# Three edits in the embedding stages of an eight-core decoder trunk: FFN tiles interleaved, norm sums on 32-column tiles, last norm shared with GpSimd

## The chip, the cores and the metric

The kernel is one launch on all eight cores of one Trainium2 chip. The metric is device time in microseconds (us) of the slowest core. TensorE does the matmuls, VectorE and GpSimd do elementwise work, ScalarE does activations and squares, and SyncE issues the output DMAs.

The chip lowers the TensorE clock of some cores in some executions. The runs list the mean granted clock of every core. A run is called slow when one die is clearly longer at a lower clock, and slow runs are left out. Even among fast runs some cores lose 0.5 to 1% of their clock. Most of this document compares *stages of one core at full clock*, that is, without such a lowering. Their times agree between cores within about 0.1 us, except in the sample block of stage two and the tail (up to 0.6 and 0.3 us).

## The reference

One inference step of a two-layer trunk with `D_MODEL` 1024 and `D_FF` 2816. Each core has one prompt of 2048 tokens and one eighth of the 1024 sample tokens. Cut to what matters:

```python
for i in range(2):
    x = x + 0.5 * swiglu(rmsnorm(x, norm_ffn[i, 0]), w_ffn_gate_up[i, 0], w_ffn_down[i, 0])
    x = x + mixer(rmsnorm(x, norm_mix[i]))
    x = x + 0.5 * swiglu(rmsnorm(x, norm_ffn[i, 1]), ...)
    # the embedding stage
    gate = sigmoid(rmsnorm(x, norm_ple[i]) @ w_ple_gate[i])
    emb  = rmsnorm(p[i] @ w_ple_proj[i], norm_ple_proj[i])
    x = x + gate * emb
y = rmsnorm(x, norm_final)
```

Every embedding stage is followed by a norm: the first by that of layer 1's FFN, the second by `norm_final`, which is the output.

## The kernel before

A core holds `x` in five blocks: `b` 0 to 3 are 512 prompt tokens each, `b` 4 (`SB`) is 128 sample tokens. Channels lie on the 128 partitions, in eight chunks (`c`, `mo`). So a norm's sum over channels is a sum over partitions: ScalarE squares a chunk, and TensorE multiplies the squares by a 128x128 matrix of ones (`ONES`, holding 1/1024), which leaves the mean in every partition of a PSUM bank.

```python
class Norm:                                    # mode "pe" alone shown
    def square():
        sq = SQ.get()
        act(sq[:, 0:n], xs, AF.Square)                         # ScalarE
        defer(self.wait * k, lambda: add(sq), self.tag)        # placed later
    def add(sq):
        if i == 0: self.pb = bank()
        mm(self.pb[:, 0:n], [(ONES[:, :], sq[:, 0:n])], start=i == 0, stop=i == 7)
        if i == 7: self.rsqrt()
    def rsqrt(self):
        rs = scr()                                             # in SBUF
        act(rs[:, 0:n], self.pb[:, 0:n], AF.Abs_reciprocal_sqrt, bias=NORM_EPS)
        def f():                                               # for c = 0..7, deferred
            out = X if self.final else H
            dve_stt(out[b][:, c, :], X[b][:, c, :], pcol(self.gname, c), rs[:, 0:n], ALU.mult, ALU.mult)
            if self.final:
                dma("sp", d_yT[:, o_:o_ + n], X[b][:, c, :], "osem")

def ple(l, gnext, ahead):                      # the embedding stage of layer l
    for mo, b in order:                        # blocks 0 and 1 mixed, then 2, 3, SB
        if mo == 0:
            if b == SB: advance(ahead, 3)      # three tiles of the next FFN
            ...
            nm[b] = Norm(b, gnext, "pe")
        mm(pz[:, 0:n], [... 8 gate matmuls ...])
        mm(pe_[:, 0:n], [... 2 embedding matmuls ...])
        act(th[:, 0:n], pz[:, 0:n], AF.Tanh, scale=0.5)
        dve_stt(th, th, 1.0, pe_, ALU.add, ALU.mult)
        dve_stt(X[b][:, mo, :], th, GPPH[...], X[b][:, mo, :], ALU.mult, ALU.add)
        nm[b].chunk(mo, 2.8)
```

The square root is in another activation table than the tanh, so each norm costs ScalarE two table loads of 1.28 us. And each of the eight norm multiplies reads two operands in SBUF, `X` and `rs`.

Of the kernel before, what the change touches and what calls it, by code (L numbers as in the profile page):

```python
# [9 lines left out]
AF = mybir.ActivationFunctionType  # L10
ALU = mybir.AluOpType
# [7 lines left out]
NSAMP = NS * TS  # L19
# [5 lines left out]
SB = NB - 1  # L25
NORM_EPS = 1e-6
# [329 lines left out]
def build_program():  # L356
# [37 lines left out]
    X = [alloc(f"x{b}", [128, 8, BLK[b]], F32, f"x{b}") for b in range(NB)]  # L394
# [4 lines left out]
    HID = [at(f"hid{b}", [128, NHP, BLK[b]], BF16, "hid", hid0 + NHP * 2 * BOFF[b], True) for b in range(NB)]  # L399
# [28 lines left out]
    ONES = alloc("ones", [128, 128], BF16)  # L428
# [19 lines left out]
    def pcol(name, c=0, n=1):  # L448
        return PAR[:, PCOL[name] + c:PCOL[name] + c + n]
# [6 lines left out]
    def defer(delay, fn, tag=None):  # L456
        seq[0] += 1
        heapq.heappush(pend, (pe_t[0] + delay, seq[0], tag, fn))
# [33 lines left out]
    def act(out, in_, func, bias=None, scale=None):  # L492
        kw = {}
        rd = [in_]
        if bias is not None:
            kw["bias"] = bias
            if not isinstance(bias, float):
                rd.append(bias)
        if scale is not None:
            kw["scale"] = scale  # L500
            if not isinstance(scale, float):
                rd.append(scale)
        tset = "abs_reciprocal_sqrt_and_small" if func == AF.Abs_reciprocal_sqrt else "silu_and_others"
        keep = func in (AF.Square, AF.Copy, AF.Identity)

        def fn(e):
            if not keep and tset != act_set[0]:
                e.preload_act_table_set(tset)  # L508
                act_set[0] = tset
            return e.activation(out=out, in_=in_, func=func, **kw)  # L510
        S.op("act", fn, reads=rd, writes=[out])
# [3 lines left out]
    def dve_tt(out, in0, in1, op):  # L515
        S.op("dve", lambda e: e.tensor_tensor(out=out, in0=in0, in1=in1, op=op), reads=[in0, in1], writes=[out])

    def pool_tt(out, in0, in1, op):
        S.op("pool", lambda e: e.tensor_tensor(out=out, in0=in0, in1=in1, op=op), reads=[in0, in1], writes=[out])  # L519

    def dve_stt(out, in0, scalar, in1, op0, op1):
        rd = [in0, in1] + ([] if isinstance(scalar, float) else [scalar])
        S.op("dve", lambda e: e.scalar_tensor_tensor(out=out, in0=in0, scalar=scalar, in1=in1, op0=op0, op1=op1),  # L523
             reads=rd, writes=[out])
# [22 lines left out]
    def mm_ops(ops):  # L547
        run_due()

        def fn(e):  # L550
            ins = None
            for i, (o_, l, r, st, sp) in enumerate(ops):
                ins = e.matmul(o_, l, r, start=st, stop=sp)  # L553
                if i == 0 and PE_FW[0] is not None:
                    ins._wait_ge(*PE_FW[0])
                    PE_FW[0] = None
            return ins
        rd = [a for op in ops for a in op[1:3]]
        wr = []
        for op in ops:  # L560
            if not any(op[0] is w for w in wr):
                wr.append(op[0])
        S.op("pe", fn, reads=rd, writes=wr)
# [7 lines left out]
    def mm(out, pairs, start=True, stop=True):  # L571
        n = len(pairs)
        mm_ops([(out, l, r, start and i == 0, stop and i == n - 1) for i, (l, r) in enumerate(pairs)])
        pe_t[0] += sum(max(width(r), 64) + 6.5 for _, r in pairs) / 2400.0
# [87 lines left out]
    class Norm:  # L662
        def __init__(self, b, gname, mode="dve"):
            self.b, self.gname, self.mode = b, gname, mode
            self.final = gname == "norm_final"
            self.n = BLK[b]
            self.tag = ("n", b)
            self.nsq = self.nadd = 0
            self.wait = {"pe": 4.0, "dve": 1.2, "pool": 1.0}[mode]

        def chunk(self, mo, lag=0.8):
            n, xs = self.n, X[self.b][:, mo, :]
            k = 1.0 if n == 512 else 0.4
            add_tt = pool_tt if self.mode == "pool" else dve_tt

            def square():
                self.nsq += 1
                if self.mode != "pe" and self.nsq == 1:
                    self.acc = scr()
                    act(self.acc[:, 0:n], xs, AF.Square)  # L680
                    return
                sq = SQ.get()
                act(sq[:, 0:n], xs, AF.Square)
                defer(self.wait * k, lambda: add(sq), self.tag)

            def add(sq):
                i = self.nadd
                self.nadd += 1
                if self.mode == "pe":
                    if i == 0:  # L690
                        self.pb = bank()
                    mm(self.pb[:, 0:n], [(ONES[:, :], sq[:, 0:n])], start=i == 0, stop=i == 7)
                    SQ.put(sq)
                    if i == 7:
                        self.rsqrt()
                elif i < 6:
                    add_tt(self.acc[:, 0:n], self.acc[:, 0:n], sq[:, 0:n], ALU.add)
                    SQ.put(sq)
                else:
                    add_tt(sq[:, 0:n], self.acc[:, 0:n], sq[:, 0:n], ALU.add)  # L700
                    sfree(self.acc)
                    defer({512: 2.5, NSAMP: 9.0}[n] + (1.5 if self.mode == "pool" else 0.0), lambda: stats(sq), self.tag)

            def stats(sq):
                self.pb = bank()
                mm(self.pb[:, 0:n], [(ONES[:, :], sq[:, 0:n])])
                SQ.put(sq)
                self.rsqrt()

            defer(lag * k, square, self.tag)  # L710

        def rsqrt(self):
            n, b = self.n, self.b
            rs = scr()
            act(rs[:, 0:n], self.pb[:, 0:n], AF.Abs_reciprocal_sqrt, bias=NORM_EPS)
            bfree(self.pb)
            st = 0.7 if n == 512 else 0.3

            def mk(c):
                def f():  # L720
                    out = X if self.final else H
                    dve_stt(out[b][:, c, :], X[b][:, c, :], pcol(self.gname, c), rs[:, 0:n], ALU.mult, ALU.mult)
                    if c == 7:
                        sfree(rs)
                    if self.final:
                        o_ = 8 * BOFF[b] + c * n
                        dma("sp", d_yT[:, o_:o_ + n], X[b][:, c, :], "osem")
                return f
            for c in range(8):
                defer(2.0 + st * c, mk(c), self.tag)  # L730
# [161 lines left out]
    def advance(gen, n=None):  # L892
        while gen is not None and n != 0:
            try:
                next(gen)
            except StopIteration:
                return
            n = None if n is None else n - 1
# [286 lines left out]
    def ple(l, gnext, ahead):  # L1185
        wp = kview(W.get(("plep", l)), 2)
        order = [(mo, b) for b in range(2) for mo in range(3)] + [(mo, b) for b in range(2) for mo in range(3, 8)]
        order += [(mo, b) for b in range(2, NB) for mo in range(8)]
        nm = {}
        for mo, b in order:  # L1190
            n = BLK[b]
            if mo == 0:
                if b == SB:
                    advance(ahead, 3)
                ensure(("n", b))
                ensure(("pt", b))
                nm[b] = Norm(b, gnext, "pe")
            ch = [c for c in TRI if mo in c][0]
            wt = kview(W.get(("pleg", l, ch)), 8)
            ii = ch.index(mo)  # L1200
            pz, pe_ = bank(), bank()
            mm(pz[:, 0:n], [(wt[:, k, ii * 128:(ii + 1) * 128], H[b][:, k, :]) for k in range(8)])
            mm(pe_[:, 0:n], [(wp[:, k, mo * 128:(mo + 1) * 128], HID[b][:, k, :]) for k in range(2)])
            th = scr()
            act(th[:, 0:n], pz[:, 0:n], AF.Tanh, scale=0.5)
            bfree(pz)
            dve_stt(th[:, 0:n], th[:, 0:n], 1.0, pe_[:, 0:n], ALU.add, ALU.mult)
            bfree(pe_)
            dve_stt(X[b][:, mo, :], th[:, 0:n], GPPH[:, l * 8 + mo:l * 8 + mo + 1], X[b][:, mo, :],
                    ALU.mult, ALU.add)  # L1210
            sfree(th)
            nm[b].chunk(mo, 2.8)
        W.done(("plep", l))
        for ch in TRI:
            W.done(("pleg", l, ch))
# [133 lines left out]
```

## Time and profile before

The median was 2630.95 us (2630.5 to 2632.32, three runs). The profiled execution was shorter, 2625.39 us; its slowest core's span is 2623.8 us.

| | us |
|---|---|
| TensorE busy | 2569.3 of 2623.8 |
| first embedding stage, with the FFN tiles run ahead in it | 128.33 |
| second embedding stage, first to last matmul | 91.16 |
| of it blocks 0 to 2, block 3, sample block | 56.77, 20.88, 13.52 |
| tail, last matmul to the end | 13.67 |

The stages are measured in each core's trace between named matmuls, as the median of the cores. These are the head, part 1 and the first line of part 4 (the chain of work that ended last) of the page of the kernel before.

```profile
span 2623.8 us, 34956 instructions; the slowest of 8 cores (2617.4 to 2623.8 us)
PE 2569.3 (98%) x14375; PEld 1245.7 (47%) x14375; DVE 1154.5 (44%) x2039; ACT 708.4 (27%) x1257; POOL 168.0 (6%) x254
...
PE 88%; DVE 5%; ACT 2%; DMA 2%; issue 1%; SPq 1%; POOL 0%; ACTq 0%; DVEq 0%; POOLq 0%
```

TensorE is the limit over the whole kernel. These are the largest waits of TensorE in the second stage, on core 0 of the kernel before (engine, line, what it waited for; us in total, times, longest us).

```profile
PE ps L553 <- DVE scr_95 L523: 3.1, 1, 3.1
PE ps L553 <- DVE scr_96 L523: 1.5, 1, 1.5
```

The TensorE timeline of the same core (start, duration, engine, line, operation, count; in brackets the idle time before it and what ended that) shows where two of such waits lie: the first three lines are block 3 of the first stage, the last the sample block of the second.

```profile
1274.58 1.90 PE L553 MATMUL ps<-h_51,ring 128*128 128x512 bf16 x8
1276.53 0.59 PE L553 MATMUL ps<-hid_56,ring 128*128 128x512 bf16 x2
1278.61 1.90 PE L553 MATMUL ps<-h_51,ring 128*128 128x512 bf16 x8 [1.49 <-DVE scr_96 L523]
...
2601.54 1.04 PE L553 MATMUL ps<-h_52,ring 128*128 128x128 bf16 x8 [3.09 <-DVE scr_95 L523]
```

In the tail, VectorE multiplies the last chunks of block 3 (128x512) and of the sample block (128x128), and SyncE issues one DMA for each. The VectorE and SyncE timelines of core 0, before:

```profile
2612.13 0.61 DVE L523 SCALAR_TENSOR_TENSOR x_47<-x_47,par,scr_93 128x128 f32<-128x128 f32 x2
2612.65 0.75 DVE L523 SCALAR_TENSOR_TENSOR x_46<-x_46,par,scr_95 128x512 f32<-128x512 f32 x1
...
2618.03 1.87 SPq L577 DMA_DIRECT2D yT<-x_46  x4
```

A 128x512 multiply takes 0.75 us, a 128x128 one 0.35, and an issue about 0.48 from start to start.

### The profile page before, as it was taken

To read this page: it belongs to the slowest core of one execution; us is meant where nothing else is said; L and a number is where in the kernel's file an instruction comes from. 1 tells how busy PE (TensorE), PEld (TensorE's weight loads), DVE (VectorE), ACT (ScalarE), POOL (GpSimd) and SP (SyncE) were. 2 spreads that over 40 slices of the span, in tenths; PEclk is the share of its full clock that TensorE was granted. 3 is DMA by queue.
4 is the path that set the end of the run, shared out by engine and by line. 5 is a ranking of instruction groups with operands and counts; after the bars stand their busy time and mean duration, and the time that the engine had idled before them with its cause. 6 is when DMAs were issued, how large, how long until landed. Compare 5 with 4: busy or idle time off the path is not lost.

```text
span 2623.8 us, 34956 instructions; the slowest of 8 cores (2617.4 to 2623.8 us)
## 1 busy us (share of the span) xinstructions
PE 2569.3 (98%) x14375; PEld 1245.7 (47%) x14375; DVE 1154.5 (44%) x2039; ACT 708.4 (27%) x1257; POOL 168.0 (6%) x254
## 2 busy tenths in 40 slices
PE   7999999999899999999999999999999999999997
PEld 3544544444454454444444454445444544544443
DVE  5432344755632222258732222267667322222687
ACT  5210112336621001124521001123334210011254
POOL 0000000012300000000000000000005000000000
PEclk9999999999999999999999999999999999999998
DMA  8220321146341123112042031102310320322113
GB/s 199 51 45 1 65 45 25 24 100 120 78 74 33 25 39 54 29 29 50 1 77 41 17 57 33 33 13 42 61 33 8 57 53 17 57 37 41 21 22 137
DMA packets 53311, 127.18 MB, mean 48 GB/s; under 512 B 9504, under 2 KB 24608, under 8 KB 53024
## 3 DMA queue, kind: packets, MB, share of 16 engines
q0 software_dynamic: 23584, 92.55, 20.4%
q1 hardware_dynamic: 28848, 31.29, 4.4%
q8 instruction: 113, 1.85, 0.3%
q10 hardware_dynamic: 720, 1.11, 0.1%
q14 instruction: 46, 0.38, 0.0%
HBM read 196.61 MB, written 10.62 MB: 79 GB/s over the span
## 4 chain that ended last, share of the span: by engine, by line
PE 88%; DVE 5%; ACT 2%; DMA 2%; issue 1%; SPq 1%; POOL 0%; ACTq 0%; DVEq 0%; POOLq 0%
PE ps L553 88%; SPq L577 1%; DMA ring<-wts 1%; ACT L508 1%; DVE h_50 L523 1%; DVE x_46 L523 0%; DVE h_51 L523 0%; DMA x_43<-xT 0%; DMA rr<-u 0%; DVE h_48 L523 0%; DVE h_49 L523 0%; POOL scr_96 L519 0%; DVE x_45 L523 0%; DVE x_43 L523 0%; DVE scr_93 L523 0%
## 5 line engine op out<-in xcount | busy, mean ns | idle before, releaser
L553 PE MATMUL ps<-h_48,ring 128*128 128x512 bf16 x1892 | 429.6, 380 | 14.4 <-DMA ring<-wts 14.4
L553 PE MATMUL ps<-h_51,ring 128*128 128x512 bf16 x1892 | 427.8, 380 | 3.2 <-DVE scr_96 L523 3.0
L553 PE MATMUL ps<-h_49,ring 128*128 128x512 bf16 x1892 | 427.7, 379 | 1.9 <-DVE h_49 L528 1.4
L553 PE MATMUL ps<-h_50,ring 128*128 128x512 bf16 x1892 | 426.2, 379 | 1.5 <-DVE h_50 L523 1.5
L553 PEld LDWEIGHTS ps<-h_51,ring 128*128 128x128 bf16 x1892 | 185.0, 98 | 228.0 <-DVE scr_96 L523 4.0
L553 PEld LDWEIGHTS ps<-h_50,ring 128*128 128x128 bf16 x1892 | 184.7, 98 | 225.3 <-DVE h_50 L523 2.0
L553 PEld LDWEIGHTS ps<-h_49,ring 128*128 128x128 bf16 x1892 | 184.4, 98 | 225.0 <-DVE h_49 L528 3.8
L553 PEld LDWEIGHTS ps<-h_48,ring 128*128 128x128 bf16 x1892 | 181.4, 98 | 220.1 <-issue 14.6
L577 POOL DMA_DIRECT2D ring<-wts x152 | 80.8, 538 | 2048.6 <-PE ps L553 1960.7
L553 PE MATMUL ps<-hid_56,ring 128*128 128x512 bf16 x736 | 163.8, 379 | 0.0
L553 PE MATMUL ps<-hid_54,ring 128*128 128x512 bf16 x736 | 163.7, 379 | 0.0
L553 PE MATMUL ps<-hid_55,ring 128*128 128x512 bf16 x736 | 163.7, 379 | 0.0
L553 PE MATMUL ps<-hid_53,ring 128*128 128x512 bf16 x736 | 162.8, 379 | 0.0
L510 ACT ACTIVATE scr_94<-ps 128x512 f32<-128x512 f32 (+1 forms) x109 | 61.6, 565 | 323.2 <-PE ps L553 322.9
L510 ACT ACTIVATE scr_97<-ps 128x512 f32<-128x512 f32 (+1 forms) x134 | 69.8, 521 | 282.4 <-PE ps L553 274.8
L510 ACT ACTIVATE scr_96<-ps 128x512 f32<-128x512 f32 (+1 forms) x120 | 68.5, 571 | 237.4 <-PE ps L553 235.2
L510 ACT ACTIVATE scr_95<-ps 128x512 f32<-128x512 f32 (+1 forms) x131 | 68.6, 524 | 234.8 <-PE ps L553 234.5
L553 PE MATMUL ps<-h_52,ring 128*128 128x128 bf16 x1892 | 124.5, 221 | 4.6 <-DVE scr_95 L523 3.1
L553 PEld LDWEIGHTS ps<-h_52,ring 128*128 128x128 bf16 x1892 | 115.3, 99 | 27.5 <-DVE scr_95 L523 3.3
L553 PEld LDWEIGHTS ps<-hid_56,ring 128*128 128x128 bf16 x736 | 72.0, 98 | 86.8
L553 PEld LDWEIGHTS ps<-hid_54,ring 128*128 128x128 bf16 x736 | 72.0, 98 | 86.6
L553 PEld LDWEIGHTS ps<-hid_55,ring 128*128 128x128 bf16 x736 | 72.0, 98 | 86.6
(490 smaller groups left out, 2171.8 us busy)
## 6 DMA issues: line engine op xcount, KB each, us to landing
ring<-wts POOLq DMA_DIRECT2D x110, 512.0 KB, 8.4
ring<-wts POOLq DMA_DIRECT2D x40, 768.0 KB, 6.4
rr<-u SPq DMA_DIRECT2D x48, 135.0 KB, 5.3
rr<-u SPq DMA_DIRECT2D x16, 134.8 KB, 3.5
x_44<-xT SPq DMA_DIRECT2D x8, 256.0 KB, 6.2
x_45<-xT SPq DMA_DIRECT2D x8, 256.0 KB, 11.2
x_46<-xT SPq DMA_DIRECT2D x8, 256.0 KB, 11.6
yT<-x_43 SPq DMA_DIRECT2D x8, 256.0 KB, 2.1
```

Source lines behind the costliest of these rows:

```text
L508: e.preload_act_table_set(tset)
L510: return e.activation(out=out, in_=in_, func=func, **kw)
L523: S.op("dve", lambda e: e.scalar_tensor_tensor(out=out, in0=in0, scalar=scalar, in1=in1, op0=op0, op1=op1), reads=rd, writes=[out])
L553: ins = e.matmul(o_, l, r, start=st, stop=sp)
L577: S.op(eng, lambda e: e.dma_start(out=out, in_=in_), reads=[in_], writes=[out], dma_sem=sem, dma_total=total, extra_deps=extra)
```

## The change

Three things, with three intents. **Tiling:** an accumulation over eight chunks makes TensorE read 8x512 columns for one row of sums. A 32-column tile of the array can sum a chunk on its own, and four such tiles hold four chunks side by side; so blocks 0 to 2 use two groups of four, and then combine the four partial sums. **Interleaving:** three more tiles of the next FFN run inside block 3 of the first stage, to give TensorE work while VectorE catches up. **Sharing:** for the last norm of prompt blocks, GpSimd does three of the eight multiplies; as the instruction used there multiplies two tensors and leaves no place for the gain, ScalarE multiplies the gain in beforehand.

```diff
+            self.shared = (2, 4, 6) if self.final and b < SB else ()
...
+            def tiled():                       # after every four squares
+                mm_ops([(self.pb[32 * q:32 * q + 32, 0:n], ONES[:, 0:32], HID[self.b][:, 3 + 4 * g + q, :], g == 0,
+                         g == 1) for q in range(4)])
+                if g == 1:
+                    hi, lo = self.hl
+                    act(hi[:, 0:n], self.pb[:, 0:n], AF.Copy)
+                    dve_tt(lo[:, 0:n], self.pb[:, 0:n], hi[:, 0:n], ALU.subtract)
+                    defer({512: 5.0, NSAMP: 2.5}[n], combine, self.tag)
+            def combine():
+                mm(self.pb[:, 0:n], [(ONES[:, :], t[:, 0:n]) for t in self.hl])
+                self.rsqrt()
...
+                if mo in self.shared:
+                    act(xs, xs, AF.Copy, scale=pcol(self.gname, mo))
...
-                    dve_stt(out[b][:, c, :], X[b][:, c, :], pcol(self.gname, c), rs[:, 0:n], ALU.mult, ALU.mult)
+                    if c in self.shared:
+                        pool_tt(X[b][:, c, :], X[b][:, c, :], rs[:, 0:n], ALU.mult)
+                    else:
+                        dve_stt(out[b][:, c, :], X[b][:, c, :], pcol(self.gname, c), rs[:, 0:n], ALU.mult, ALU.mult)
...
-                nm[b] = Norm(b, gnext, "pe")
+                nm[b] = Norm(b, gnext, "tile" if b < 3 else "pe")
+            if b == 3 and mo in (3, 5, 7):
+                advance(ahead, 1)
```

Cut: the housekeeping of buffers (tiled blocks keep their squares in free rows of `HID`), and the square root's `scale=32.0` (each partial sum stands in 32 partitions and is divided by 1024 a second time). `hi` and `lo` split the partial sums into two bfloat16 values, so that combining loses little precision.

More of the change, by code (lines that the diff above doesn't have):

```diff
@@ L667, in __init__ @@
             self.tag = ("n", b)
+            self.shared = (2, 4, 6) if self.final and b < SB else ()
             self.nsq = self.nadd = 0
-            self.wait = {"pe": 4.0, "dve": 1.2, "pool": 1.0}[mode]
+            self.wait = {"pe": 4.0, "tile": 5.0, "dve": 1.2, "pool": 1.0}[mode]
         def chunk(self, mo, lag=0.8):
@@ L674, in chunk, with square_ @@
             add_tt = pool_tt if self.mode == "pool" else dve_tt
+            def tiled():
+                g = self.nadd
+                self.nadd += 1
+                if g == 0:
+                    self.pb = bank()
+                mm_ops([(self.pb[32 * q:32 * q + 32, 0:n], ONES[:, 0:32], HID[self.b][:, 3 + 4 * g + q, :], g == 0,
+                         g == 1) for q in range(4)])
+                pe_t[0] += (n + 26) / 2400.0
+                if g == 1:
+                    self.hl = [SQ.get(), SQ.get()]
+                    hi, lo = self.hl
+                    act(hi[:, 0:n], self.pb[:, 0:n], AF.Copy)
+                    dve_tt(lo[:, 0:n], self.pb[:, 0:n], hi[:, 0:n], ALU.subtract)
+                    bfree(self.pb)
+                    defer({512: 5.0, NSAMP: 2.5}[n], combine, self.tag)
+            def combine():
+                self.pb = bank()
+                mm(self.pb[:, 0:n], [(ONES[:, :], t[:, 0:n]) for t in self.hl])
+                for t in self.hl:
+                    SQ.put(t)
+                self.rsqrt()
             def square():
+                square_()
+                if mo in self.shared:
+                    act(xs, xs, AF.Copy, scale=pcol(self.gname, mo))
+            def square_():
                 self.nsq += 1
+                if self.mode == "tile":
+                    act(HID[self.b][:, 2 + self.nsq, :], xs, AF.Square)
+                    if self.nsq % 4 == 0:
+                        defer(self.wait * k, tiled, self.tag)
+                    return
                 if self.mode != "pe" and self.nsq == 1:
@@ L714, in rsqrt @@
             rs = scr()
-            act(rs[:, 0:n], self.pb[:, 0:n], AF.Abs_reciprocal_sqrt, bias=NORM_EPS)
+            act(rs[:, 0:n], self.pb[:, 0:n], AF.Abs_reciprocal_sqrt, bias=NORM_EPS,
+                scale=32.0 if self.mode == "tile" else 1.0)
             bfree(self.pb)
```

## The prediction

> **What bounds the kernel.** TensorE. The page gives PE 98% busy of a 2623.8 us span, and 88% of the chain of work that ended last; the granted clock is 0.994. The change touches only the two embedding stages (about 1216-1316 us and 2519-2610 us in the PE timeline) and the tail after them. There the PE timeline has 512-column matmuls every 0.216 us without gaps, except these stalls, all behind VectorE. Stage one: 1.49 us in block 3, then 0.51, 0.76, 0.46 and 0.48 in the sample block (3.7 us). Stage two: 1.49 us in block 3, 0.64 and 3.09 us in the sample block, and behind the 3.09 a half-clock stretch (8 sample matmuls every 0.83 us instead of 0.45) that costs about 2 us. The 3.09 and 1.49 stalls come from VectorE: in its timeline it waits 3.2 us for ScalarE (two 1.28 us table loads around each norm's square root) and then works off a backlog with eight 0.67 us norm multiplies mixed in. The tail, from the last matmul to the end, is 13.5 us; its 16 output DMA issues stand one behind the other every 0.48 us.
>
> **What the change does to TensorE.** Per block of 0 to 2, eight ones-matmuls (8 x 0.216 = 1.73 us) become two groups of four 32-column matmuls plus two combining ones. The Trainium skill, page "TensorEngine Tiling (Array Packing)", section "Key Properties", says that changing the tiling mode drains TensorE, and that column tiles run in parallel. The trace agrees: the convolution's 32-column groups of four cost 0.22 us each, with about 0.1 us more on entering and on leaving. So 2 x 0.42 + 0.43 = 1.26 us, a gain of 0.47 us per block, 2.8 us over six. It lies on the path, since TensorE has no gaps there. The norms end some 6 us later, which nobody waits for, except that block 2's last norm moves into the sample block.
>
> **Interleaving.** Six FFN tiles run before the sample block instead of three; nothing is added. Each is 3.45 us of TensorE for one 0.7 us VectorE operation, so block 3's 1.49 us stall goes. The sample block's 2.2 us stay mostly: block 3's norm still falls there. Gain 1.5 to 2.
>
> **Last norm shared.** Three of eight multiplies per prompt block leave VectorE (2 us per block); ScalarE pays three copies of about 0.6 us and GpSimd three multiplies of 1.15 us or more. The Trainium skill, page "GPSIMD Engine Reference", table in section 1, says that SBUF interfaces are shared with VectorE and contended with two SBUF inputs; the trace agrees: five norm multiplies took 0.92 us each beside GpSimd work, which then took 1.7. So about half of the relief remains. It removes the 1.49 us stall of block 3 and part of the 3.09 and of the half clock: 3 us (1 to 6), the later norm of block 2 working against it. The tail stays bound by the DMA issues: 0.6 us.
>
> **Sum.** 2.8 + 1.7 + 3 + 0.6, about 8 us: 2623 us, range 2617.5 to 2629. Faster by over 2%: 0.005; within 2%: 0.99; slower: 0.005.
>
> **Right or wrong in the profile.** 32-column groups of 0.3 to 0.45 us start to start; no stall over 1 us in either block 3; the sample block of stage two shorter by 1 to 4 us at full clock; still about 13 us after the last matmul, with issues every 0.48 us.
>
> **What would make it wrong.** Column groups that don't overlap (0.8 us each) would turn the gain into a loss. Table loads of block 2's later norm just before the sample block could starve TensorE there again. GpSimd contention could slow VectorE by as much as it relieves.

## The result, and the profile after

The changed kernel took 2631.93 us (median of four runs, 2630.63 to 2633.4), the kernel before 2631.64 us (2630.5 to 2632.41) beside it. The ratio of the fast runs is 1.0002, with a 95% interval of 0.9984 to 1.0019: the same. Ratios here are the mean time of one kernel's fast runs over that of the other's in the same rounds, so they are not quite the ratio of the quoted medians. The predicted 2623.0 us, and its range of 2617.5 to 2629, were missed.

The first suspicion must be the clock. The views of all cores (median of each die) are, before and then after:

```profile
die 0 (median of its cores): 2621.4 us, clock 0.994
die 1 (median of its cores): 2621.8 us, clock 0.995
```

```profile
die 0 (median of its cores): 2621.7 us, clock 0.994
die 1 (median of its cores): 2628.1 us, clock 0.990
```

Die 1 did lose clock in the changed kernel's four runs. But die 0, at the same clock in both, shows no gain either: 2621.7 against 2621.4 us. So the missing 8 us are not hidden by the clock. They are missing in the stages:

| core at full clock, us | stage 1 | stage 2 (blocks 0-2 / block 3 / sample) | tail | sum |
|---|---|---|---|---|
| before | 128.33 | 91.16 (56.77 / 20.88 / 13.52) | 13.67 | 233.16 |
| after (die 0) | 126.62 | 90.15 (55.22 / 20.21 / 14.72) | 15.99 | 232.76 |
| difference | -1.71 | -1.01 | +2.32 | -0.40 |

The long stretch between the stages is the same in every kernel, 1174.90 us. From the page after:

```profile
PE 2563.0 (97%) x14133; PEld 1245.7 (47%) x14387; DVE 1155.2 (44%) x2033; ACT 719.4 (27%) x1275; POOL 182.8 (7%) x266
```

The weight loads rose by 12, as the change adds two matmuls to each of six norms; that the matmuls seem to have fallen by 242 means that records are missing from this trace. VectorE's busy time did not fall, although 12 multiplies were taken from it and only 6 small subtractions added; GpSimd's rose by 14.8 us for 12 instructions. The waits of TensorE in stage two, core 0 after:

```profile
PE ps L553 <- DVE scr_94 L523: 1.9, 2, 1.5
PE ps L553 <- ACT scr_95 L510: 1.5, 1, 1.5
PE ps L553 <- ACT sq_91 L510: 1.1, 1, 1.1
```

The one wait of 3.1 us has become several smaller ones, some of them for ScalarE. TensorE's timeline after shows the column groups (`ones 128*32`), first one within a stretch without a wait, then one in the first stage that waits for VectorE:

```profile
1239.66 1.89 PE L553 MATMUL ps<-h_49,ring 128*128 128x512 bf16 x8
1241.48 0.40 PE L553 MATMUL ps<-hid_53,ones 128*32 128x512 bf16 x4
1241.81 0.61 PE L553 MATMUL ps<-hid_54,ring 128*128 128x512 bf16 x2
...
1271.70 0.40 PE L553 MATMUL ps<-hid_55,ones 128*32 128x512 bf16 x4 [1.22 <-DVE scr_93 L523]
```

The group takes 0.33 us from start to start, with 0.09 us more ahead of it: 1239.66 plus eight times 0.216 is 1241.39, not 1241.48. That is 0.42 us, as predicted. And this is the tail after, from the VectorE, GpSimd and SyncE timelines of core 0:

```profile
2609.12 0.75 DVE L523 SCALAR_TENSOR_TENSOR x_46<-x_46,par,scr_97 128x512 f32<-128x512 f32 x1
2609.79 3.89 DVE L523 SCALAR_TENSOR_TENSOR x_47<-x_47,par,scr_94 128x128 f32<-128x128 f32 x3
...
2609.23 4.30 POOL L519 TENSOR_TENSOR x_46<-x_46,scr_97 128x512 f32<-128x512 f32 x3 [11.16 <-ACT scr_97 L510]
...
2611.21 2.87 SPq L577 DMA_DIRECT2D yT<-x_47  x3
...
2617.25 2.46 SPq L577 DMA_DIRECT2D yT<-x_46  x5
```

Three VectorE multiplies of 128x128, which took 0.61 us for two before, take 3.89 us here, while GpSimd works through its three. SyncE, which follows VectorE in order, issues three DMAs in 2.87 us.

The sizes behind those sums are in the view of one source line (count, then nanoseconds least, median, most). Before and after, the same multiply:

```profile
L523 DVE SCALAR_TENSOR_TENSOR x_47<-x_47,par,scr_93 x8: 347/347/348, 2612.1 to 2616.0; 128x128 f32<-128x128 f32 x8
```

```profile
L523 DVE SCALAR_TENSOR_TENSOR x_47<-x_47,par,scr_94 x3: 1344/1345/1351, 2609.8 to 2612.3; 128x128 f32<-128x128 f32 x3
```

**Theory.** Tiling pays on TensorE where TensorE is the limit. Sharing gives that back in the tail, because an instruction of VectorE with two SBUF operands cannot run beside GpSimd's: it waits for GpSimd's whole instruction. Interleaving does nothing for the stall it aimed at. **Rivals.** In the tail: GpSimd's multiply is slow in itself and its result arrives late (dependence), or the output queue is the limit. In the sample block of stage two: the later norm of block 2, with its table loads, against TensorE merely arriving earlier at work that VectorE and ScalarE set the pace of.

### The profile page after: what moved, and what is told of

Read it like the earlier page. It is cut to its first block, busy times and chain, and to the rows that moved or that the text cites. A ratio compares the mean times of both kernels' runs of the same rounds, so it can differ in the third digit from the quotient of the medians.

```text
span 2631.9 us, 34689 instructions; the slowest of 8 cores (2617.2 to 2631.9 us)
## 1 busy us (share of the span) xinstructions
PE 2563.0 (97%) x14133; PEld 1245.7 (47%) x14387; DVE 1155.2 (44%) x2033; ACT 719.4 (27%) x1275; POOL 182.8 (7%) x266
## 4 chain that ended last, share of the span: by engine, by line
PE 89%; DVE 4%; ACT 2%; DMA 2%; issue 1%; SPq 1%; POOL 0%; DVEq 0%; ACTq 0%; POOLq 0%
PE ps L553 89%; SPq L577 1%; ACT L508 1%; DVE h_50 L523 1%; DMA x_43<-xT 0%; DVE x_46 L523 0%; DMA xscr_69<-st_sc 0%; DMA rr<-u 0%; DVE h_48 L523 0%; POOL scr_96 L519 0%; DVE h_49 L523 0%; DMA x_44<-xT 0%; DMA ring<-wts 0%; DVE x_45 L523 0%; DVE x_47 L523 0%
## 5 line engine op out<-in xcount | busy, mean ns | idle before, releaser
L553 PEld LDWEIGHTS ps<-h_49,ring 128*128 128x128 bf16 x1892 | 185.7, 98 | 229.2 <-issue 16.4
L553 PEld LDWEIGHTS ps<-h_50,ring 128*128 128x128 bf16 x1892 | 185.1, 98 | 227.0 <-issue 9.4
L553 PEld LDWEIGHTS ps<-h_51,ring 128*128 128x128 bf16 x1892 | 185.2, 98 | 225.8 <-issue 6.9
L553 PEld LDWEIGHTS ps<-h_48,ring 128*128 128x128 bf16 x1892 | 182.1, 98 | 222.0 <-issue 24.4
L510 ACT ACTIVATE scr_96<-ps 128x512 f32<-128x512 f32 (+1 forms) x124 | 70.5, 569 | 370.2 <-PE ps L553 366.5
L510 ACT ACTIVATE scr_97<-ps 128x512 f32<-128x512 f32 (+1 forms) x131 | 69.1, 527 | 284.9 <-PE ps L553 277.4
L510 ACT ACTIVATE scr_95<-ps 128x512 f32<-128x512 f32 (+1 forms) x131 | 68.3, 521 | 234.8 <-PE ps L553 234.8
L553 PEld LDWEIGHTS ps<-h_52,ring 128*128 128x128 bf16 x1892 | 115.4, 99 | 25.8 <-DVE scr_94 L523 1.9
L553 PEld LDWEIGHTS ps<-hid_56,ring 128*128 128x128 bf16 x736 | 72.0, 98 | 86.7
L553 PEld LDWEIGHTS ps<-hid_55,ring 128*128 128x128 bf16 x736 | 71.9, 98 | 86.8 <-issue 0.5
L553 PEld LDWEIGHTS ps<-hid_54,ring 128*128 128x128 bf16 x736 | 71.7, 98 | 86.9 <-issue 1.8
L553 PEld LDWEIGHTS ps<-hid_53,ring 128*128 128x128 bf16 x736 | 71.6, 98 | 84.1 <-issue 0.2
```

Source lines behind the costliest of these rows:

```text
L510: return e.activation(out=out, in_=in_, func=func, **kw)
L553: ins = e.matmul(o_, l, r, start=st, stop=sp)
```

## The experiments

All kernels gave correct results. Stages are given as in the table above; the edits are against the changed kernel unless said otherwise. Where one look is quoted as a time, its profile fell in the fast state; where the kernel before beside it was slow (2938 us in the first group), only stages are compared.

### Tiling alone

```diff
-            self.shared = (2, 4, 6) if self.final and b < SB else ()
+            self.shared = ()
-            if b == 3 and mo in (3, 5, 7):
-                advance(ahead, 1)
```

> Only the column tiling of the square sums is kept; no interleaving, no sharing. Measured on the four cores of the die at full clock, before and after are: first embedding stage (with the twelve or nine lead FFN tiles after it) 128.3 and 126.6 us; second stage 91.2 and 90.15 us, of it blocks 0 to 2 56.8 and 55.2, block 3 20.9 and 20.2, sample block 13.5 and 14.7; tail after the last matmul 13.7 and 16.0. My theory: the tail's loss of 2.3 us comes from the sharing alone (GpSimd and VectorE shut each other out of SBUF), so the tail is 13.7 (13.2 to 14.2) here. Rival: the tail's loss comes from the later end of the tiled norms, which pushes block 2's output writes into the tail; then it stays near 16. First stage: tiling saves 12 matmuls of 0.216 less 12 mode changes of 0.1, 1.4 us, so 126.9 (126.4 to 127.4) if no new stall comes with it.

Measured (one look, 2624.5 us): stage 1 126.19, stage 2 91.48 (56.51 / 19.31 / 15.67), tail 13.48, sum 231.15: 2.0 us less than before. The tail is back, so the tail's loss is not the tiling's. Stage 1 gained 2.14 us. Stage 2 gained nothing: blocks 0 to 2 are only 0.26 us shorter, block 3 is 1.57 us shorter, and the sample block 2.15 us longer. At the end of blocks 0 to 2 a column group now waits for VectorE, just ahead of block 3's first gate matmul (core 0):

```profile
2571.38 0.40 PE L553 MATMUL ps<-hid,ones 128*32 128x512 bf16 x4 [1.21 <-DVE scr L523]
```

### Everything but the tiling

```diff
-                nm[b] = Norm(b, gnext, "tile" if b < 3 else "pe")
+                nm[b] = Norm(b, gnext, "pe")
```

> Interleaving and sharing are kept, the square sums are as before. First stage: the interleaving was forecast to take away block 3's 1.5 us stall, which gives 126.8; the after trace shows new stalls of 1.3 and 0.7 us in its place, so my theory now is that the interleaving alone gives less than 0.7 us (127.6 to 128.4). Second stage: the sharing without tiling; block 2's norm is then not late, so if the late norm causes the longer sample block (14.7 for 13.5), it is 13.0 or less here; if GpSimd causes it, it stays at 14.5 or more. Tail: 16.0 by the theory that sharing costs it, 13.7 by the rival that tiling does.

Measured (2628.3 us): stage 1 127.94, stage 2 91.04 (57.71 / 19.61 / 13.7), tail 16.41, sum 235.39: 2.2 us *more* than before. The sample block's 13.7 us lie between the brackets of 13.0 and 14.5, so this run doesn't tell the late norm from GpSimd there. Interleaving gives 0.39 us in stage 1; sharing costs 2.7 us in the tail and gains 0.1 in stage 2. The 1.49 us stall that interleaving was to remove is unchanged in this kernel's TensorE timeline (core 0):

```profile
1273.88 1.90 PE L553 MATMUL ps<-h,ring 128*128 128x512 bf16 x8 [1.49 <-DVE scr L523]
```

### No sharing in block 3

```diff
-            self.shared = (2, 4, 6) if self.final and b < SB else ()
+            self.shared = (2, 4, 6) if self.final and b < SB - 1 else ()
```

> The changed kernel with the sharing taken from block 3 alone, whose norm stands in the tail. Theory (VectorE and GpSimd exclude each other): tail 13.3 to 14.0 for 16.0, second stage as in the changed kernel, 90.1. Rival (the tail's cost is in the order of the sample block's norm before block 3's, or in the output writes): tail stays within 0.5 us of 16.0.

Measured (2623.3 us): stage 1 126.64, stage 2 89.33 (55.22 / 20.20 / 13.91), tail 13.52, sum 229.49. The whole loss of the tail belongs to block 3's three GpSimd multiplies. The sample block is 0.8 us shorter as well. Sharing in blocks 0 to 2 does pay: stage 2 is 2.15 us shorter than with tiling alone. In those blocks only one VectorE instruction per block was caught, `x<-scr,gpph,x`, with 1.2 to 1.75 us; the others beside GpSimd are those with a PSUM operand.

### The last norms' reciprocal root in PSUM

For block 3 and the sample block, the root is written back into the bank of its sums, and VectorE's multiplies read it there. GpSimd keeps its own copy in SBUF and its three multiplies.

```diff
+            inps = self.final and b >= SB - 1
+            rv, pb = rs, self.pb
...
+            if inps:
+                rv = pb
+                act(rv[:, 0:n], pb[:, 0:n], AF.Abs_reciprocal_sqrt, bias=NORM_EPS)
...
-                        dve_stt(out[b][:, c, :], X[b][:, c, :], pcol(self.gname, c), rs[:, 0:n], ALU.mult, ALU.mult)
+                        dve_stt(out[b][:, c, :], X[b][:, c, :], pcol(self.gname, c), rv[:, 0:n], ALU.mult, ALU.mult)
```

Cut: the root into `rs`, which the sample block now leaves out, and the freeing of the bank.

> The changed kernel; only the place is changed from which VectorE reads the reciprocal root in the last norms of block 3 and of the sample block: a PSUM bank (ScalarE writes it a second time, 0.6 us), so that each of these VectorE multiplies has one SBUF tensor input instead of two. Data split, GpSimd work and order of outputs stay. Theory (two SBUF tensor inputs on VectorE and GpSimd exclude each other): no VectorE multiply of the tail takes over 0.8 us (in the changed kernel three of 0.34 us took 1.35 us each), GpSimd's take 1.16 us, and the tail is 12.8 to 14.0 us. Rival (a dependency or the queue of output writes holds them): three VectorE operations of over 1.2 us remain and the tail stays at 15.5 or more.

Measured (2623.9 us): tail 14.10 instead of 15.99, stages as after (126.62, 90.21). The source view of the multiplies and the GpSimd timeline, core 0:

```profile
L523 DVE SCALAR_TENSOR_TENSOR x<-x,par,ps x13: 342/343/747, 2609.1 to 2614.7; 128x128 f32<-128x128 f32 x8, 128x512 f32<-128x512 f32 x5
```

```profile
2609.76 3.72 POOL L519 TENSOR_TENSOR x<-x,scr 128x512 f32<-128x512 f32 x3 [11.16 <-ACT scr L510]
```

Both engines work at the same time, and no VectorE multiply takes over 0.75 us. GpSimd does as many multiplies as before, on the same data, and the outputs depend on it as before. So dependence on GpSimd is not what cost the 1.9 us that came back. It is VectorE's second SBUF operand. The tail is still 0.6 us longer than without sharing in block 3 (13.52, above); VectorE waits 0.77 us here for ScalarE's second root (core 0, before the multiply at 2610.26 us).

### Three GpSimd multiplies that nobody needs

On the kernel *before*, at the square root of block 3's last norm; in the second kernel with a copy of one operand instead.

```diff
+            if self.final and b == SB - 1:
+                for _ in range(3):
+                    pool_tt(XSCR[1][:, 0:n], X[0][:, 0, :], rs[:, 0:n], ALU.mult)
```

> The kernel before, with three GpSimd multiplies of two SBUF inputs into a tile that nobody reads, released by block 3's reciprocal root in the tail. Nothing waits for them by data. Theory (GpSimd and VectorE exclude each other when both read two SBUF tensors): three VectorE multiplies take 1.3 us and more, and the tail grows from 13.7 to 15.7 to 17.5 us. Rival (the tail of the changed kernel was longer by its order and dependencies): tail 13.7, within 0.3.

```diff
-                    pool_tt(XSCR[1][:, 0:n], X[0][:, 0, :], rs[:, 0:n], ALU.mult)
+                    pool_copy(XSCR[1][:, 0:n], rs[:, 0:n])
```

> As e6, but three GpSimd copies of one SBUF input. If it takes two inputs on GpSimd to hold VectorE up, the tail stays at 13.7 within 0.3 and VectorE's multiplies at 0.75 us; if any GpSimd access to SBUF does, some of VectorE's multiplies take over 1 us and the tail grows by 1 us or more.

Measured: tail 16.16 with the multiplies, 14.23 with the copies, 13.67 before. VectorE's and GpSimd's lines of the first, core 0:

```profile
L523 DVE SCALAR_TENSOR_TENSOR x<-x,par,scr x16: 337/737/1744, 2609.6 to 2619.4; 128x512 f32<-128x512 f32 x8, 128x128 f32<-128x128 f32 x8
```

```profile
2609.70 4.95 POOL L519 TENSOR_TENSOR xscr<-x,scr 128x512 f32<-128x512 f32 x3 [91.66 <-ACT scr L510]
```

The output doesn't depend on these multiplies, and still the tail is 2.5 us longer: presence alone costs it. With copies one 128x512 multiply of VectorE took 1.09 us instead of 0.75, and two 128x128 ones 0.70 and 0.69 instead of 0.35 (core 0). So a GpSimd instruction with one SBUF input holds such a multiply up too, by 0.34 to 0.35 us each. The tail's 0.56 us are less than the 1 us that was expected for that case.

### Block 2 of the second stage not tiled

Tiling alone, with this edit beside it:

```diff
-                nm[b] = Norm(b, gnext, "tile" if b < 3 else "pe")
+                nm[b] = Norm(b, gnext, "tile" if b < 3 - l else "pe")
```

> The tiling alone, as in e1, but in the second embedding stage only for blocks 0 and 1; block 2 keeps the old square sums there. In e1 the second stage took 91.5 us (before: 91.2), of it the sample block 15.7 (before: 13.5), so the 1.4 us that tiling saves were given back. Theory: the tiled norm of block 2 ends later, its two table loads fall just before the sample block and starve it; then the sample block is back at 13.8 or less, block 3 at 19.8 to 20.5, and the stage at 90.0 to 90.7. Rival: the sample block is longer because TensorE arrives earlier at work that VectorE bounds anyway; then block 3 and sample block together stay at 35.0 us (e1: 19.3 and 15.7) within 0.3.

Two cores were at 13/16 of the clock for long in this run (about 140 and 175 us); the others give stage 2 90.91 (55.66 / 20.89 / 14.36). From the start of block 3 to the last matmul that is 35.25 us, against 34.98 with block 2 tiled and 34.40 before: the sample block is 1.3 us shorter than with block 2 tiled, but block 3 is 1.6 us longer. As it was sized, the theory of the late norm and its table loads falls. The whole stage is 0.57 us shorter than with block 2 tiled, so tiling block 2 does cost something in this kernel, ahead of block 3: the wait of 1.21 us is gone.

What stays is that these 35 us are set by VectorE and ScalarE, whenever TensorE arrives there: with sharing in blocks 0 to 2, which relieves VectorE, the same stretch took 34.11 us. The run holds an unplanned test of it as well. On core 0 the clock was lowered for 22.7 us within this stretch (its window, then busy time and count of PE, PEld, DVE, ACT, POOL, PEclk, DMA share, GB/s):

```profile
2578.10:2600.80 22.70, 19.67 (x96) 9.08 (x96) 19.26 (x30) 10.97 (x17) 0.00 (x0) 0.81 0.45 169
```

Block 3 took 22.80 us there instead of 20.89, but the whole stretch 35.4 instead of 35.25: a slower TensorE hardly moves its end. In blocks 0 to 2, where TensorE is the limit, 4.9 us at the same lowered clock made the changed kernel's core 4 0.87 us longer (56.09 for 55.22).

### Interleaving earlier

On the kernel before:

```diff
+            if b == 3 and mo in (1, 3, 5):
+                advance(ahead, 1)
```

> The kernel before with the interleaving alone, but ahead of tiles 1, 3 and 5 of block 3 instead of 3, 5 and 7. In e2 the interleaving left the 1.5 us stall where it was, ahead of the matmuls of tile 2, since its first FFN tile comes after it. Theory: an FFN tile ahead of tile 1 gives VectorE the time to catch up, the stall is gone and the first stage takes 126.4 to 127.1 us (before 128.3, e2 127.9). Rival (the stall is ScalarE's table loads and moves along): 127.7 or more, with a stall of over 1 us at another place.

Measured: stage 1 128.08 instead of 128.33. TensorE's timeline, core 0:

```profile
1270.80 3.83 PE L553 MATMUL ps<-h,ring 128*128 128x512 bf16 x16 [0.17 <-DVE scr L523]
1276.19 0.39 PE L553 MATMUL ps<-sq,ones 128*128 128x512 bf16 x1 [1.56 <-ACT sq L510]
```

The FFN tile (the 16 matmuls) now stands ahead of `mo` 1, and there is no stall ahead of `mo` 2 any more. But TensorE works in program order: right behind the tile it stands 1.56 us at a ones-matmul that needs a square from ScalarE. The stall moved. The square was late because its input came from the same backlog of VectorE: ScalarE sat idle 2.86 us for that input, which VectorE wrote only after four norm multiplies in a row (ScalarE's line, then VectorE's).

```profile
1275.51 0.63 ACT L510 ACTIVATE sq<-x 128x512 bf16<-128x512 f32 x1 [2.86 <-DVE x L523]
1271.36 2.73 DVE L523 SCALAR_TENSOR_TENSOR h<-x,par,scr 128x512 bf16<-128x512 f32 x4
```

### Tiling, with sharing in blocks 0 to 2 only, and the change again

The first kernel is without the interleaving and with block 3 unshared; the second is the changed kernel unmodified.

> What the experiments leave of the change: tiling of blocks 0 to 2, sharing of the last norm for blocks 0 to 2 only, no interleaving. By the stages measured on cores at full clock: first stage 126.2 us (e1), second stage 89.3 and tail 13.5 (e3), together 4.1 us under the kernel before (128.3, 91.2, 13.7). Theory that the parts act stage by stage and don't meet: these three numbers within 0.3 us. Rival: without the interleaving block 3 and the norms of the first stage behave otherwise, and the sum of the three is over 230 us. The whole time should be 0.1 to 0.2% under the kernel before, which the clock of single runs may hide.

> The changed kernel again, on the same chip and in the same rounds as e9. By its stages on cores at full clock it should stand 0.4 us under the kernel before, so a ratio of 1.000 within 0.001. If the equal times of the first result came only from a lower clock on one die that hid a gain of 8 us, the ratio is 0.997 here.

Measured: the first has stage 1 126.27, stage 2 89.34, tail 13.48, sum 229.09, which is 4.1 us less than before, and 0.4 less than with the interleaving (229.49). The changed kernel repeated its stages within 0.15 us (126.76, 90.08, 15.98). The verdicts of these five rounds are wide, since runs with two cores at lowered clock (about 2650 us) count as fast: ratio 0.9996 (0.9936 to 1.0057), and 0.9997 (0.9931 to 1.0062). If one looks at those executions alone in which all cores had a mean clock of at least 0.993, the kernel before took 2627.2 us (median of 7), the changed kernel 2625.1 to 2625.6 (3), and this one 2622.1 (median of 4). This selection was made after the fact, and it puts the changed kernel some 1.8 us under the kernel before where the stages say 0.4; the stages are the firmer evidence.

### The sample block's outputs issued by a second queue

The kernel just above, with:

```diff
-                        dma("sp", d_yT[:, o_:o_ + n], X[b][:, c, :], "osem")
+                        dma("act" if b == SB else "sp", d_yT[:, o_:o_ + n], X[b][:, c, :], "osem")
```

> e9, with the sample block's eight output writes of the tail issued by ScalarE's queue instead of SyncE's. If the tail is bound by the sixteen issues of 0.48 us on one queue, as forecast, it falls from 13.5 to 11.5 us or less; if VectorE's sixteen multiplies (7.5 us) bound it too, it falls by 0.1 to 0.7 us only.

> The kernel of e10 again, timed. Its stages on cores at full clock were 126.3, 89.3 and 12.5 us, 5.1 us under the kernel before. Executions in which no core has a lowered clock should take 2621 to 2622 us, 5 to 6.5 us under the kernel before in the same rounds; if the stages don't add up to the whole time, less than 3 us.

The second is the same kernel, timed. Measured: tail 12.49, twice: 1.0 us shorter, where the theory of the queue as the only limit wanted more and that of VectorE as the only limit less. Both bind: half the issues leave SyncE, and then VectorE's multiplies set the end. The sum of stages is 228.07, 5.1 us less than before. The timed ratio is 1.0023 (0.9972 to 1.0075), again with executions at lowered clock in it, and says nothing either way. With all cores at 0.993 or more the executions were 2621.57, 2621.93 and 2624.12 us, one of three above the expected 2621 to 2622, and the kernel before's 2625.8 to 2627.4 (8). It is the best version that was found, by some 0.2%, on the evidence of stages and of that selection.

## Why the prediction was wrong

In the undisturbed sums of stages, the 8 us expected became 0.4 us:

| term | predicted | measured (sum of stages) |
|---|---|---|
| tiling | -2.8 | -2.0 (tiling alone) |
| interleaving | -1.7 | +0.4 (229.49 - 229.09: sharing in blocks 0 to 2, with and without it) |
| sharing, stage two | -3 | -1.3 (90.15 - 91.48) |
| sharing, tail | -0.6 | +2.5 (15.99 - 13.48) |

**"So about half of the relief remains", and the tail's 0.6 us: the costliest step.** The prediction read five norm multiplies beside GpSimd as 0.92 us each and took that for a slowdown of all. It was an average over two kinds: in the trace they took 1.04, 0.74, 1.64, 0.74 and 0.74 us. These lines of the kernel *before*, core 3, in which VectorE and GpSimd overlap, could have told it; first VectorE's, then GpSimd's:

```profile
2023.20 1.64 DVE L523 SCALAR_TENSOR_TENSOR h_50<-x_45,par,scr_93 128x512 bf16<-128x512 f32 x1
2024.77 0.68 DVE L516 TENSOR_TENSOR x_46<-ps,x_46 128x512 f32<-128x512 f32 x1
2025.37 4.59 DVE L523 SCALAR_TENSOR_TENSOR h_50<-x_45,par,scr_93 128x512 bf16<-128x512 f32 x5
...
2024.50 1.36 POOL L519 TENSOR_TENSOR scr_96<-scr_96,sq_90 128x512 f32<-128x512 f32 x1 [0.20 <-POOL scr_96 L519]
```

A multiply with two SBUF operands took 1.64 us, and the next instruction, with an operand in PSUM, took 0.68, in the midst of GpSimd's 1.36. Over that core, the two-SBUF multiply takes 0.745 us in the median free (221 of them) and 1.42 where GpSimd's adds overlap it by over 0.4 us (19, from 0.74 to 1.72), while `x<-ps,x` takes 0.69 beside them and 0.68 free. The Trainium skill, page "SBUF — State Buffer", section "SBUF: two separate sides", says that the port pair of VectorE and GpSimd is an exclusive lock and not a shared bandwidth, which a VectorE instruction with two SBUF inputs needs against a GpSimd instruction that reads SBUF, and that the other "fully blocks". A multiply of 0.35 us took 1.34 to 1.35 us, that is about one of GpSimd's (4.30 us for three); with a PSUM operand it took 0.34. The prediction cited only the page "GPSIMD Engine Reference", which calls it contention, and sized it as if the loss were shared. In the tail, where VectorE and the queue behind it are the chain, three lockouts of 1.0 us each (1.345 - 0.347) are of the size of the 2.5 us.

**"It lies on the path, since TensorE has no gaps there": true in one stage of two.** The group's cost (0.42 us) and the saving per block (0.47 us) were right. In stage 1 the gain was 2.14 us, more than the 1.41 us of three blocks; TensorE's waits there are 0.35 us shorter in sum (3.94 and 3.59 on core 0), and the rest was not traced. In stage 2 tiling alone gained nothing. "No gaps" held for blocks 0 to 2 of the kernel before; with the tiling in, a column group waits 1.21 us for VectorE at their end, so they gained 0.26 us and not 1.41. Behind them stand block 3 and the sample block, whose waits were in the same timeline: from the start of block 3 the time left is set by VectorE and ScalarE (34.4 us before, 35.0 with tiling), so what TensorE saves earlier is waited for later. Only with VectorE relieved by sharing in blocks 0 to 2 did this stage gain. That the two edits help one another, the prediction did not see. Nor did the half clock go, from which part of the 3 us was to come: core 0 has a window of 6.83 us of it in the sample block of both kernels. It was also worth less than the 2 us that the prediction gave it: in the kernel before, core 4 had 3.41 us less of it, and its sample block was 0.3 to 0.6 us shorter than the others'.

**"So block 3's 1.49 us stall goes": it was misplaced.** The stall lies ahead of `mo` 2's matmuls, and the first of the added tiles stands behind them, ahead of `mo` 3's. Reading the position in the timeline against the loop would have shown it. And where the tile does stand ahead of it, a stall of 1.56 us behind ScalarE takes its place. In the changed kernel the 1.49 us stall is gone in stage 1, but through the tiling; a column group waits 1.22 us in its place, and with interleaving another wait is 0.65 us instead of 0.30. Against tiling alone these two waits are 0.44 us longer (1.22 + 0.65 against 1.13 + 0.30), which is the 0.4 us that the interleaving costs there.

**What was right.** Column groups start to start within 0.3 to 0.45 us. Block 3's stall in stage two is no longer over 1 us (0.45 and 0.38 are left). Issues stand every 0.48 us where VectorE keeps ahead. What was not right beside the steps above: the sample block was predicted shorter by 1 to 4 us and is longer by 1.2. Of this, 0.4 us are there with tiling and sharing in blocks 0 to 2 alone (13.91 against 13.52), and 0.8 come with sharing block 3 (14.72 against 13.91). The risks named in the prediction, block 2's table loads and GpSimd's lock, are both seen there (TensorE waits 1.5 us for ScalarE right behind a table load, one VectorE multiply takes 1.2 us), but their shares of the 0.4 us are not shown. The 0.8 us go through ScalarE's copies, which the prediction counted but put on no path. One copy stands ahead of the first table load; here are both in the changed kernel, then the same load without sharing in block 3 (core 0).

```profile
2591.10 0.72 ACT L510 ACTIVATE x_46<-x_46,par 128x512 f32<-128x512 f32 x1
2592.32 1.28 ACT L508 ACT_TABLE_LOAD   x1
...
2592.36 1.28 ACT L508 ACT_TABLE_LOAD   x1
```

Stage two began at 2517.05 and 2517.84 us, so the load came 75.27 us into the stage with the copy and 74.52 without it. From the load to the last matmul both kernels took 14.8 us.

## What to carry to other kernels

Work moved from VectorE to GpSimd is free only beside VectorE instructions that don't need the shared SBUF ports: list what will run beside it by operand, read the *longest* duration of such pairs rather than a mean, and put one operand in PSUM where that is not so. A saving on the busiest engine counts only up to the next point where it waits for another, so follow the waits behind the saving to the end of the stage before adding it up. And look up on which side of a stall the filling work will stand in program order, since in-order engines fill a gap only with what is ahead of it.

## What the Trainium skill lacked or had wrong

- "ScalarE: Activation LUTs", section "What ACT_TABLE_LOAD costs": it gives about 1283 ns for the load and 1380 ns of drain, 2.66 us for a switch. The load agrees; the drain isn't seen. In ScalarE's timeline of the changed kernel, core 0, the next activation starts 1.29 us after the load's start:

```profile
2607.03 1.28 ACT L508 ACT_TABLE_LOAD   x1
2608.32 0.28 ACT L510 ACTIVATE scr_94<-ps 128x128 f32<-128x128 f32 x1
```

- "TensorE: Matmul & The Clock Gate", Part 1: it says that three cores of a die with dense matmuls bring the die to 13/16 of the clock, for as long as the load lasts. Slow executions agree: in one of the changed kernel (3068.27 us) the cores of die 1 had a mean clock of 0.83 to 0.84. In fast ones it doesn't hold: four cores per die run dense matmuls (97 to 98% busy on the slowest core) at a mean clock of 0.99. There a lowered clock comes mostly in windows of 4 to 10 us, as in this window of the changed kernel, core 4, in which core 0 has 1.00 (span, busy time and count of PE, PEld, DVE, ACT, POOL, then PEclk, DMA share, GB/s); in some executions two cores stay lowered for long.

```profile
1224.00:1233.00 9.00, 9.00 (x37) 3.79 (x36) 8.86 (x15) 6.62 (x11) 0.00 (x0) 0.82 1.00 147
```

- "TensorEngine Tiling (Array Packing)", section "Key Properties": it says that changing the mode drains TensorE, and gives no size. The runs show 0.09 us on entering a group of four 32-column matmuls of 512 columns (1241.48 - 1241.39) and 0.11 us on leaving (0.33 us from start to start less the 0.216 of one full matmul, if the four run side by side).
- "SBUF — State Buffer", section "SBUF: two separate sides": the lock is described for a VectorE instruction with two SBUF inputs against GpSimd reading SBUF, and the runs bear it out, also for a GpSimd copy with one input (a multiply of 0.35 us took 0.70 beside it). The page has no figure for such a pair; three copies cost the tail 0.56 us here, three multiplies 2.5 us.
